# Two feed-forward stages on TensorE: one more pair per group with seven products instead of eight, more low parts made by adding transfers through a load buffer of their own, and the first squares moved

## The chip, the cores and the metric

The kernel runs on one NeuronCore of one Trainium2 chip. The metric is the time of one execution in microseconds (us), as the device measures it. Three runs of the kernel before took 2454.0, 2455.01 and 2455.87 us: median 2455.01. One further execution was profiled; all rows of the trace come from it.

## What is computed

One layer of a streaming encoder block on a residual stream `x` of 256 tokens by 2048 features, in float32:

```python
x = x + 0.5 * swiglu(rms_norm(x, ffn1_norm), ffn1_w_up, ffn1_w_down)
h = rms_norm(x, mix_norm)
...                    # gated recurrence, RG-LRU branch, gates, w_out
x = x + cross_attention(rms_norm(x, xattn_norm), rms_norm(mem, mem_norm), wq, wkv, wo)
x = x + 0.5 * swiglu(rms_norm(x, ffn2_norm), ffn2_w_up, ffn2_w_down)
return rms_norm(x, final_norm)

def swiglu(h, w_up, w_down):
    gate, up = jnp.split(h @ w_up, 2, axis=-1)
    return (jax.nn.silu(gate) * up) @ w_down
```

The change lies in the two feed-forward (SwiGLU) stages; the hidden width is 5632. What stands between them keeps its instructions and gets only other pools for three small tiles.

## The kernel before

**Precision.** TensorE multiplies in float32r, a shortened float32. Each float32 operand is therefore split into a high part `h` (a copy on ScalarE, `split`, L120) and a low part `l` (the raw value minus `h`, on VectorE, L121). A product of two split operands is three matmuls: high by high and high by low (L449, L450), and low by high (L452). 512 columns are written by each.

**Pieces.** The weights arrive from HBM in pieces of 128 by 2048 numbers (1 MB). `plan` lists all of them in their order of use; `weights()` hands out a piece and starts the preparation of the next one, so the program is written one piece ahead of its use. Buffers come in rings: three `raw`, three `h`, three `l` of 2048 columns, and in the feed-forward stages three `wide` ones.

**Groups and pairs.** The hidden features are worked off in 11 groups of 512 (`NG`). For a group, eight up pieces (pairs `p` = 0 to 7) are multiplied with the normed tokens, and their sums make gate and up. A pair is a 2 by 2 block product, for which `PRODUCTS` holds three recipes. `plain` (group 0) and `mixed` use eight products of plain weight blocks, 24 matmuls. `fast` uses seven products, 21 matmuls, and sums of weight blocks: VectorE makes the sums `td` in three operations (L213 to L215), and the sums are split too, into `th` (two copies on ScalarE; the trace calls the tile `h`) and `tl` (two operations on VectorE, 1024 columns each). The tokens' side needs differences (`less`) for `mixed` and sums for `fast`, both from `operand_pairs`/`sums` (L432); `BOTH` lists the pairs that need both.

**Order.** `ffn_order` writes the pieces of a stage. In groups 1 and 2 the pairs alternate between `mixed` and `fast`, four each. From group 3 on the order of pairs is 1, 3, 0, 4, 2, 6, 5, 7, with 0 and 6 `mixed` and the rest `fast`. Behind the pairs of a group stand down pieces of earlier groups (two in groups 1 and 2, then four; 24 matmuls each, always eight pieces for a block of two groups), whose sums are added to the residual (L561). At a group's end VectorE combines the seven sums, activates, and the result is turned on TensorE (L489) and split (`hidop`).

**Added pieces.** For `mixed` pieces after the first one of group 3 VectorE does not make the low part. `begin_added` (L187 to L193) runs one piece earlier: it loads a raw buffer, ScalarE writes `-raw`, rounded, into `l` (L191), and a transfer issued by GpSimd (POOL) adds `raw` to it (L192); `prepare` later copies the high part (L200). There are 15 such pieces in a stage.

**Scheduling.** The framework's scheduler then moves instructions within each engine's queue, TensorE's matmuls too, after costs of its own; each engine runs its queue strictly in the order that results. Only SyncE, ScalarE and VectorE are kept in written order during the first eight pieces. There `head` and `rest` (L600 to L606) say what is done ahead of and behind each piece: loading and splitting the tokens (`head_x`), loading the residual and squaring it on ScalarE (`head_residual`, two column blocks at a time behind pieces 4 and 5), the tokens' sums, and the root of the mean square (`head_rstd`, behind piece 8).

Of the kernel before, what the change touches and what calls it, by code (L numbers as in the profile page):

```python
# [8 lines left out]
F32 = mybir.dt.float32  # L9
# [32 lines left out]
def ffn_order():  # L42

    out, down = [("plain", 0, p) for p in range(8)], [("down", 0, 1, c, 0) for c in range(4)]
    for g in range(1, NG):
        if g < 3:  # L50
            out += [(("mixed", "fast")[p % 2], g, p) for p in (0, 1, 2, 3, 5, 4, 7, 6)]
        else:
            out += [("mixed" if p in (0, 6) else "fast", g, p) for p in (1, 3, 0, 4, 2, 6, 5, 7)]
        if g > 2 and g % 2:
            down = [("down", g - 2, 2, c, b) for c in range(4) for b in (g - 2, g - 1)]
        n = 2 if g < 3 else 4
        out, down = out + down[:n], down[n:]
    return out + [("down", NG - 2, 2, c, b) for c in range(4) for b in (NG - 2, NG - 1)]
# [3 lines left out]
def block_kernel(ctx: ExitStack, tc: tile.TileContext, xT, xin, memT, vec, gfin, bgate, lruw, wu1, wd1, win, wv,  # L62
# [123 lines left out]
    def begin_added(src):  # L186

        raw = rawp.tile([P, 2048], F32, name="raw", tag="raw")
        l = lp.tile([P, 2048], F32R, name="l", tag="l")
        sp.dma_start(raw, src)  # L190
        act.activation(l, raw, ACT.Copy, scale=-1.0)  # L191
        nc.gpsimd.dma_start(l, raw, accum_op=ALU.add)  # L192
        return raw, l  # L193
# [111 lines left out]
    class Squares:  # L305
# [3 lines left out]
        def add(self, src):  # L309
            if self.ss is None:  # L310
                self.ss = small.tile([P, T], F32, name="ss", tag="ss")
                act.activation(self.ss, src, ACT.Square)
            else:
                s = t1("sq")
                act.activation(s, src, ACT.Square)
                dve.tensor_tensor(out=self.ss, in0=self.ss, in1=s, op=ALU.add)

        def rstd(self):
# [5 lines left out]
            r = small.tile([P, T], F32, name="rstd", tag="rstd", bufs=3)  # L324
# [15 lines left out]
    FFN_POOLS = dict(wide=3, hd=1)  # L340

    class TokenSquares:
# [5 lines left out]
        def add(self, c, ts=range(2)):  # L348
            for t in ts:
                name = "hd" if "hd" in scoped else "tmp2"  # L350
                junk = scoped[name].tile([P, 512], F32, name="junk", tag=name)
# [20 lines left out]
    def by_feature(r):  # L372
# [7 lines left out]
        o = small.tile([P, T], F32, name="rstd", tag="rstd", bufs=3)  # L380
# [22 lines left out]
    BOTH = [2, 4]  # L403
    xd = []

    def operand_pairs(src, gain, q, xg, out):

        for a in src:
# [7 lines left out]
            less = None if i else (h[:, 512:768], l[:, 512:768])  # L416
# [7 lines left out]
        def sums(which=((0, "less"), (0, "sums"), (1, "less"), (1, "sums"))):  # L424
            s = slot(name="xs")
            for i, ((h, l), less) in enumerate(out):
# [10 lines left out]
                if (i or 2 * q in BOTH) and (i, "sums") in which:  # L437
                    if not i and len(which) > 1:
                        s = slot(name="xs")
# [148 lines left out]
    def head_residual(i):  # L588
        for c in (2 * i, 2 * i + 1):
            for t in range(2):  # L590
                sp.dma_start(xt[c][:, t * 512:(t + 1) * 512], xin[t * P:(t + 1) * P, c * 512:(c + 1) * 512])
            sq1.add(c)
        if i:
# [11 lines left out]
    for q, i in enumerate((3, 6, 7, 9)):  # L605
        rest[i] = lambda q=q: sums1[q](((0, "less"), (1, "sums")))  # L606
    rest[8] = head_rstd
    for q, i in ((1, 17), (2, 18)):
# [56 lines left out]
    middle.enter_context(scope(tmp=8, tmp2=2, scores=1, extra=2))  # L665
# [523 lines left out]
```

## Time and profile before

| | before |
|---|---|
| median of 3 runs | 2455.01 us (2454.0 to 2455.87) |
| the profiled execution, and its span | 2456.57 us, 2454.8 us |
| granted TensorE clock, mean | 0.997 |
| adding transfers (POOL issues) | 30, of 1024 KB each |
| DMA moved | 507.59 MB, mean 207 GB/s |
| q0 (the adding transfers' queue) | 6.4% of 16 engines' span |
| q1 (the loads' queue) | 53.4% |

The profile names an engine's instruction by its line, what it writes and what it reads. PE is TensorE's matmul, PEld its weight load, DVE is VectorE, ACT is ScalarE, SP is SyncE, which issues the loads. A duration is that of one instruction alone; instructions that follow each other directly overlap by some 0.08 us, so that a chain of them is shorter than its sum. The first feed-forward stage takes up about the first 650 us, the second about the last 700.

### The profile page before, as it was taken

The numbers are of one execution on the slowest core, as the hardware profiler recorded it, in microseconds if no ns is written. First come the engines' busy times: TensorE is split into PE (matmuls) and PEld (weight loads), VectorE is DVE, ScalarE is ACT, GpSimd is POOL, SyncE is SP. The second block draws the span as 40 slices with busy tenths as digits, with TensorE's granted clock in tenths as the row PEclk, the third lists the DMA queues.
The fourth block names the chain that finished last, engine by engine and source line by source line (L and its number), as shares of the span: only waits on it lengthen the run. The fifth ranks groups of instructions, "written<-read, shape, count | busy, mean of one in ns | idle before, by whom it ended". The sixth has DMA issues, their size and how long they took to land.

```text
span 2454.8 us, 30191 instructions
## 1 busy us (share of the span) xinstructions
PE 2434.6 (99%) x12250; PEld 2036.9 (83%) x12250; DVE 1894.1 (77%) x2016; ACT 1391.2 (57%) x1398; POOL 28.3 (1%) x36
## 2 busy tenths in 40 slices
PE   9999999999999999999999999999999999999998
PEld 7887888888888888888888888888888788888887
DVE  6998999999865757567665676556689999999995
ACT  7555666666564454477434554555555566666664
POOL 0000000000000000000000000000000000000000
PEclk9999999999999999999999999999999999999999
DMA  7557777777655445546555555444555677777774
GB/s 278 190 203 234 248 235 235 234 239 239 223 183 194 173 172 180 174 166 228 194 188 177 210 198 189 172 172 155 189 189 189 209 238 239 240 240 235 235 235 152
DMA packets 75020, 507.59 MB, mean 207 GB/s; under 512 B 8320, under 2 KB 8576, under 8 KB 15232
## 3 DMA queue, kind: packets, MB, share of 16 engines
q1 hardware_dynamic: 69840, 473.06, 53.4%
q0 software_dynamic: 4320, 31.46, 6.4%
q8 instruction: 96, 1.57, 0.2%
q10 hardware_dynamic: 720, 1.13, 0.1%
q14 instruction: 44, 0.36, 0.0%
HBM read 472.07 MB, written 2.10 MB: 193 GB/s over the span
## 4 chain that ended last, share of the span: by engine, by line
PE 95%; DVE 2%; ACT 1%; DMA 1%; issue 0%; SPq 0%; ACTq 0%; DVEq 0%
PE acc L449 17%; PE acc L450 17%; PE acc L452 17%; PE acc L231 11%; PE acc L252 8%; PE acc L253 8%; PE acc L255 8%; PE acc L235 5%; DMA raw<-wu 1%; PE acc L489 1%; ACT h L120 1%; DVE l L121 1%; PE acc L389 1%; PE acc L765 0%; PE acc L1048 0%; PE acc L1003 0%
## 5 line engine op out<-in xcount | busy, mean ns | idle before, releaser
L121 DVE TENSOR_TENSOR l<-raw,h 128x2048 fp32r<-128x2048 f32 (+2 forms) x422 | 878.0, 2087 | 364.5 <-ACT h L120 353.0
L120 ACT ACTIVATE h<-raw 128x2048 fp32r<-128x2048 f32 (+2 forms) x422 | 736.7, 1753 | 637.5 <-PE acc L253 204.8
L449 PE MATMUL acc<-h,xh 128*128 128x512 f32 x1280 | 501.2, 392 | 7.1 <-ACT h L120 7.0
L450 PE MATMUL acc<-h,xl 128*128 128x512 f32 x1280 | 499.7, 391 | 0.0
L120 ACT ACTIVATE h<-td 128x1024 fp32r<-128x1024 f32 x224 | 229.6, 1055 | 178.4 <-PE acc L450 131.0
L252 PE MATMUL acc<-h,ops 128*128 128x512 f32 x832 | 326.9, 393 | 0.0
L253 PE MATMUL acc<-h,ops 128*128 128x512 f32 x832 | 324.3, 390 | 0.0
L121 DVE TENSOR_TENSOR tl<-td,h 128x1024 fp32r<-128x1024 f32 x224 | 267.4, 1221 | 33.6 <-ACT h L120 31.0
L449 PEld LDWEIGHTS acc<-h,xh 128*128 128x128 f32 x1280 | 241.7, 189 | 60.0 <-ACT h L120 9.7
L450 PEld LDWEIGHTS acc<-h,xl 128*128 128x128 f32 x1280 | 241.9, 189 | 50.1
L231 PE MATMUL acc<-ops,h 128*128 128x512 f32 x1152 | 278.0, 393 | 0.3
L449 PE MATMUL acc<-h,hidop 128*128 128x512 f32 x704 | 275.7, 392 | 0.0
L450 PE MATMUL acc<-h,hidop 128*128 128x512 f32 x704 | 274.3, 390 | 0.0
L231 PEld LDWEIGHTS acc<-ops,h 128*128 128x128 f32 x1152 | 211.9, 188 | 42.9 <-DVE ops L292 0.9
L452 PE MATMUL acc<-l,xh 128*128 128x512 f32 x832 | 218.9, 390 | 0.0
L255 PE MATMUL acc<-l,ops 128*128 128x512 f32 x832 | 206.1, 390 | 0.0
L452 PE MATMUL acc<-l,hidop 128*128 128x512 f32 x704 | 188.3, 389 | 0.0
L452 PEld LDWEIGHTS acc<-l,xh 128*128 128x128 f32 x832 | 156.5, 188 | 32.6
L255 PEld LDWEIGHTS acc<-l,ops 128*128 128x128 f32 x832 | 156.2, 188 | 32.4
L252 PEld LDWEIGHTS acc<-h,ops 128*128 128x128 f32 x832 | 156.2, 188 | 32.3
L253 PEld LDWEIGHTS acc<-h,ops 128*128 128x128 f32 x832 | 156.3, 188 | 31.6
L452 PEld LDWEIGHTS acc<-l,hidop 128*128 128x128 f32 x704 | 132.2, 188 | 27.5
(220 smaller groups left out, 2347.6 us busy)
## 6 DMA issues: line engine op xcount, KB each, us to landing
raw<-wu SPq DMA_DIRECT2D x172, 1024.0 KB, 4.8
raw<-wd SPq DMA_DIRECT2D x88, 1024.0 KB, 4.8
raw<-win SPq DMA_DIRECT2D x40, 1024.0 KB, 4.8
raw<-wg SPq DMA_DIRECT2D x32, 1024.0 KB, 4.8
l<-raw POOLq DMA_DIRECT2D x30, 1024.0 KB, 7.3
raw<-wab SPq DMA_DIRECT2D x16, 1024.0 KB, 4.8
raw<-wout SPq DMA_DIRECT2D x16, 1024.0 KB, 4.8
raw<-wq SPq DMA_DIRECT2D x16, 1024.0 KB, 4.8
```

The costliest lines, as they stand in the source:

```text
L120: done["high"] = act.activation(h, raw, ACT.Copy).ins
L121: dve.tensor_tensor(out=l, in0=raw, in1=h.bitcast(F32), op=ALU.subtract)
L231: pe.matmul(acc, h[:, k * P:(k + 1) * P], xs[k], start=k == 0, stop=False)
L235: done["product"] = pe.matmul(acc[:, :T], l[:, k * P:(k + 1) * P], xs[k][:, :T], start=False, stop=k == KT - 1).ins
L252: pe.matmul(accs[t], x[:, t * P:][:, :P], h[j], start=first and j == 0, stop=False)
L253: pe.matmul(accs[t], x[:, T + t * P:][:, :P], h[j], start=False, stop=False)
L255: done["product"] = pe.matmul(accs[t], x[:, t * P:][:, :P], l[j], start=False, stop=last and j == 3).ins
L389: pe.transpose(accs[m // 2][:, m % 2 * T + t * P:][:, :P], tile[:, t * 512 + m * P:][:, :P], ident)
L449: pe.matmul(acc, ah, bh, start=start, stop=False)
L450: pe.matmul(acc, al, bh, start=False, stop=False)
L452: pe.matmul(acc, ah, bl, start=False, stop=stop)
L489: pe.transpose(acc[:, z * T + t * P:][:, :P], hid[t][:, (2 * y + z) * P:][:, :P], ident)
```

## The change

`ffn_order` makes one more pair `fast` in each group but the first: in groups 1 and 2 pairs 0, 2 and 6 stay `mixed` (four before), from group 3 on only pair 6 (two before). From group 3 on the order of pairs is now 1, 3, 0, 6, 4, 2, 5, 7. `plan_ffn` marks as `added` every `mixed` piece but pair 0, in groups 1 and 2 as well, and four of the eight down pieces of the blocks that begin at groups 1, 3, 5 and 7, two in a group: 28 added pieces in a stage where there were 15. `begin_added` loads into a pool `own` with one buffer. In the start, the residual's column blocks are loaded and squared one at a time, behind pieces 4, 5, 6 and 7, and the tokens' sums and the root follow behind pieces 7, 8 and 9. Pair 4 needs only sums now (`FAST`), pairs 0 and 2 both kinds. The junk output of the squares takes a `wide` buffer, and `ss`, `rstd` come from a pool of the middle part.

```diff
     for g in range(1, NG):
         if g < 3:
-            out += [(("mixed", "fast")[p % 2], g, p) for p in (0, 1, 2, 3, 5, 4, 7, 6)]
+            out += [("mixed" if p in (0, 2, 6) else "fast", g, p) for p in (0, 1, 2, 3, 5, 4, 7, 6)]
         else:
-            out += [("mixed" if p in (0, 6) else "fast", g, p) for p in (1, 3, 0, 4, 2, 6, 5, 7)]
+            out += [("mixed" if p == 6 else "fast", g, p) for p in (1, 3, 0, 6, 4, 2, 5, 7)]
...
-            kind = "fast" if e[0] == "fast" else "added" if e[0] == "mixed" and e[1:] > (3, 0) else "plain"
+            kind = "fast" if e[0] == "fast" else "plain"
+            if e[0] == "mixed" and e[2]:
+                kind = "added"
+            if e[0] == "down" and 0 < e[1] < NG - 2 and (e[3] + e[4] - e[1]) % 2 == 0:
+                kind = "added"
...
     def begin_added(src):
-        raw = rawp.tile([P, 2048], F32, name="raw", tag="raw")
+        raw = scoped["own"].tile([P, 2048], F32, name="own", tag="own")
         l = lp.tile([P, 2048], F32R, name="l", tag="l")
         sp.dma_start(raw, src)
         act.activation(l, raw, ACT.Copy, scale=-1.0)
...
-    FFN_POOLS = dict(wide=3, hd=1)
+    FFN_POOLS = dict(wide=3, own=1)
...
-    BOTH = [2, 4]
+    BOTH = [0, 2]
+    FAST = [4]
...
-    for i in range(2):
-        rest[4 + i] = lambda i=i: head_residual(i)
...
+    for i in range(3):
+        rest[4 + i] = lambda i=i: head_residual(i)
+    for q, i in enumerate((3, 7, 8, 9)):
+        rest[i] = lambda q=q: sums1[q](((0, "sums" if 2 * q in FAST else "less"), (1, "sums")))
+    made = rest[7], rest[8]
+    rest[7] = lambda: [f() for f in (lambda: head_residual(3), made[0])]
+    rest[8] = lambda: [f() for f in (head_rstd, made[1])]
+    for q, i in ((0, 22), (1, 24)):
         rest[i] = lambda q=q: sums1[q](((0, "sums"),))
```

**Three places in the order.** The first is ScalarE in the first pieces, from the high part of piece 4 on. `junk` are the squares of the residual `x0` to `x3`, `xg` and `xh` the tokens' side. Before:

```order
L120 ACTIVATE h_304<-raw_303 128x2048
L352 ACTIVATE junk_311,sst_103<-x0_99 128x512
L352 ACTIVATE junk_313,sst_103<-x0_99 128x512
L352 ACTIVATE junk_317,sst_103<-x1_100 128x512
L352 ACTIVATE junk_319,sst_103<-x1_100 128x512
L412 ACTIVATE xg_295<-xf_294,vt_76 128x256 x2
L120 ACTIVATE xh_348<-xg_295 128x512
L120 ACTIVATE h_353<-raw_352 128x2048
```

And now:

```order
L120 ACTIVATE h_304<-raw_303 128x2048
L358 ACTIVATE junk_311,sst_103<-x0_99 128x512
L358 ACTIVATE junk_313,sst_103<-x0_99 128x512
L419 ACTIVATE xg_295<-xf_294,vt_76 128x256 x2
L120 ACTIVATE xh_342<-xg_295 128x512
L120 ACTIVATE h_347<-raw_346 128x2048
L358 ACTIVATE junk_354,sst_103<-x1_100 128x512
L358 ACTIVATE junk_356,sst_103<-x1_100 128x512
```

Two squares stand between two high parts where four stood, and the same goes on for pieces 6 and 7. (On SP the first load into `own` now stands ahead of the loads for the third piece.)

The second place is a `fast` piece that is followed by an added one, in a later group of the first stage. ScalarE before (`h_2796`, `h_2800` are the piece's `h` and `th`, `h_2827` is the added piece's high part, `h_2856` belongs to the piece after that):

```order
L120 ACTIVATE h_2796<-raw_2790 128x1536
L120 ACTIVATE h_2800<-td_2792 128x1024 x2
L200 ACTIVATE h_2827<-raw_2785 128x2048
L120 ACTIVATE h_2856<-raw_2850 128x1536
L120 ACTIVATE h_2860<-td_2852 128x1024 x2
```

ScalarE now (`h_2777` is the `th`, `h_2804` the added piece's high part, `h_2833` the next piece's):

```order
L120 ACTIVATE h_2777<-td_2769 128x1024
L204 ACTIVATE h_2804<-own_2762 128x2048
L120 ACTIVATE h_2833<-raw_2827 128x1536
L120 ACTIVATE h_2777<-td_2769 128x1024
L120 ACTIVATE h_2837<-td_2829 128x1024 x2
```

TensorE now, in the same piece (`l_2774`, `tl_2778` its low parts):

```order
L456 MATMUL acc_2738<-h_2777,xh_119 128x512
L457 MATMUL acc_2738<-h_2777,xl_120 128x512
L459 MATMUL acc_2734<-l_2774,xh_119 128x512
L459 MATMUL acc_2735<-l_2774,xh_119 128x512
L459 MATMUL acc_2736<-l_2774,xh_119 128x512
L459 MATMUL acc_2737<-tl_2778,xh_119 128x512
L459 MATMUL acc_2738<-tl_2778,xh_119 128x512
L456 MATMUL acc_2735<-h_2804,xh_387 128x512
L457 MATMUL acc_2735<-h_2804,xl_388 128x512
L456 MATMUL acc_2735<-h_2804,xh_387 128x512
L456 MATMUL acc_2739<-h_2777,xh_119 128x512
L457 MATMUL acc_2739<-h_2777,xl_120 128x512
```

The second half of `th` has moved behind the next high part on ScalarE, which writes the buffer that the piece's own first six matmuls read; on TensorE its matmuls have moved behind the low parts and three matmuls of the added piece. The last piece of each group has the same shape, with a down piece in place of the added one.

The third place is SP at the start of group 3 of the first stage. Before, from the load of pair 1 on (`L207` loads a piece whose low part VectorE makes in one operation, `L210` a `fast` piece, `L190` an added one):

```order
L210 DMA raw_1270<-wu1 128x2048
L210 DMA raw_1314<-wu1 128x2048
L207 DMA raw_1374<-wu1 128x2048
L210 DMA raw_1401<-wu1 128x2048
L190 DMA raw_1441<-wu1 128x2048
L210 DMA raw_1446<-wu1 128x2048
L210 DMA raw_1506<-wu1 128x2048
```

And now (`L194` an added piece):

```order
L194 DMA own_1394<-wu1 128x2048
L214 DMA raw_1290<-wu1 128x2048
L214 DMA raw_1334<-wu1 128x2048
L214 DMA raw_1399<-wu1 128x2048
L214 DMA raw_1459<-wu1 128x2048
L214 DMA raw_1499<-wu1 128x2048
L194 DMA own_1573<-wd1 128x2048
```

The added piece's load stands outside the ring of the three `raw` buffers and ahead of the group's other loads; five `fast` pieces follow each other in the ring where an added one stood among them.

More of the change, by code (lines that the diff above doesn't have):

```diff
@@ L415, in operand_pairs @@
             split(h[:, :512], l[:, :512], g)
-            less = None if i else (h[:, 512:768], l[:, 512:768])
+            less = None if i or 2 * q in FAST else (h[:, 512:768], l[:, 512:768])
             if 2 * q + i in BOTH:
@@ L436, in sums @@
                     made(*less, 2, 0, lambda o: ((a[0], a[1], ALU.subtract), (a[2], a[3], ALU.subtract)))
-                if (i or 2 * q in BOTH) and (i, "sums") in which:
-                    if not i and len(which) > 1:
+                if (i or 2 * q in BOTH + FAST) and (i, "sums") in which:
+                    if not i and less and len(which) > 1:
                         s = slot(name="xs")
@@ L586, in head_x, with head_residual @@
         pairs1.append(out[-1])
[L588 to L593, printed above, removed]
+    def head_residual(c):
+        for t in range(2):
+            sp.dma_start(xt[c][:, t * 512:(t + 1) * 512], xin[t * P:(t + 1) * P, c * 512:(c + 1) * 512])
+        sq1.add(c)
+        if c == 3:
             sp.dma_start(vt[:, small_n:NVEC], vec[:, small_n:])
     head += [lambda p=p: head_x(p) for p in range(8)]
-    for i in range(2):
-        rest[4 + i] = lambda i=i: head_residual(i)
     rstd1 = []
```

18 lines of the change are left out of this document (8 added, 10 removed).

## The prediction, made blind

> **What bounds the kernel now.** I read the page's busy shares and chain first, then the table by windows, the list of what PE waited for, and the timelines of the two feed-forward stages. The chain of waits is PE almost throughout:
>
> ```profile
> PE 2434.6 (99%) x12250; PEld 2036.9 (83%) x12250; DVE 1894.1 (77%) x2016; ACT 1391.2 (57%) x1398; POOL 28.3 (1%) x36
> PE 95%; DVE 2%; ACT 1%; DMA 1%; issue 0%; SPq 0%; ACTq 0%; DVEq 0%
> 762.12 1.81 PE acc L255 x8
> 767.56 1.81 PE acc L255 x8
> ```
>
> The last two rows, from the chain in order of time, are one place in two neighbouring pieces of 24 matmuls: 5.44 us, so 0.2267 us for a matmul of 512 columns. A matmul less is worth that wherever PE does not wait. The windows show where it does, and how full DVE is there (columns: PE, weight load, DVE, ACT, POOL busy, clock, DMA share):
>
> ```profile
> 0.00:50.00 50.00, 45.83 (x200) 37.95 (x200) 27.38 (x46) 39.48 (x72) 0.20 (x4) 0.97 0.79 298
> 50.00:100.00 50.00, 49.41 (x221) 40.70 (x222) 49.03 (x59) 32.06 (x30) 0.00 (x0) 1.00 0.58 210
> 150.00:200.00 50.00, 46.63 (x199) 37.05 (x198) 44.71 (x48) 25.94 (x23) 1.00 (x1) 0.97 0.58 196
> 1900.00:1950.00 50.00, 46.97 (x203) 38.13 (x203) 44.03 (x41) 29.77 (x25) 0.87 (x1) 0.97 0.66 218
> 265.66:327.75 62.09, 62.09 (x279) 51.50 (x279) 57.34 (x56) 38.36 (x32) 1.76 (x2) 1.00 0.74 243
> ```
>
> The last row is one whole later group of the first stage: PE never idle, DVE busy 57.34 of 62.09 us. The period is that of the adding transfers:
>
> ```profile
> 289.13 0.89 POOL L192 DMA_DIRECT2D l<-raw  x1 [45.19 <-ACT l L191]
> 351.22 0.86 POOL L192 DMA_DIRECT2D l<-raw  x1 [45.09 <-ACT l L191]
> ```
>
> So PE sets the end, but in these stages DVE is 92% full, and the change gives DVE more and PE less. The few waits of PE, in brackets:
>
> ```profile
> 42.09 0.66 PE L449 MATMUL acc<-h,xh 128*128 128x512 f32 x1 [2.50 <-ACT h L120]
> 50.59 0.50 PE L449 MATMUL acc<-h,xh 128*128 128x512 f32 x1 [1.17 <-ACT h L120]
> 183.08 0.50 PE L449 MATMUL acc<-h,xh 128*128 128x512 f32 x1 [0.36 <-ACT h L120]
> 191.41 0.50 PE L449 MATMUL acc<-h,xh 128*128 128x512 f32 x1 [3.02 <-ACT h L120]
> 1928.36 0.73 PE L452 MATMUL acc<-tl,xh 128*128 128x512 f32 x2 [3.03 <-DVE tl L121]
> 42.00:44.00 2.00, 1.91 (x5) 1.52 (x6) 1.93 (x1) 0.04 (x1) 0.00 (x0) 0.57 0.00 0
> 44.00:46.00 2.00, 2.00 (x7) 1.58 (x6) 1.48 (x6) 0.42 (x1) 0.00 (x0) 0.58 0.23 29
> 192.00:194.00 2.00, 2.00 (x7) 1.62 (x6) 1.97 (x4) 0.57 (x1) 0.00 (x0) 0.62 1.00 422
> 194.00:196.00 2.00, 2.00 (x6) 1.52 (x6) 1.80 (x2) 1.54 (x2) 0.00 (x0) 0.53 0.53 143
> ```
>
> After 2.50 and 3.02 us of idleness the granted clock is near half for some 4 us (0.57, 0.58; 0.62, 0.53), which costs 0.425 x 3.9 = 1.66 and 0.38 x 2 + 0.47 x 2 = 1.70 us more. The wait at 50.59, 1.17 us long, has no such sequel. I take 1.7 for the one at 1928 too. Price of all waits: head 2.50 + 1.17 + 1.66 = 5.3; first stage 0.36 + 3.02 + 1.70 = 5.1; second stage 3.03 + 1.7 = 4.7; together 15.1 us.
>
> **Products.** Seven instead of eight means 21 matmuls instead of 24. Groups 1 and 2 get one more such pair each, groups 3 to 10 one more each: 10 a stage, 20 in all, 60 matmuls fewer: 60 x 0.2267 = **-13.6 us**. This term I hold for sure, since the diff's table says it outright.
>
> **DVE in a later group.** The rows for the operations, and one seven-product piece from its first operation to that of the next (298.25 to 304.78 us, 6.53 us):
>
> ```profile
> 298.25 1.22 DVE L213 TENSOR_TENSOR td<-raw 128x1024 f32<-128x1024 f32 x1
> 304.78 1.22 DVE L213 TENSOR_TENSOR td<-raw 128x1024 f32<-128x1024 f32 x1
> 269.00 4.49 DVE L121 TENSOR_TENSOR l<-raw,h 128x2048 fp32r<-128x2048 f32 x2 [0.52 <-ACT h L120]
> ```
>
> Two low parts in a row take 4.49, so 2.2 each. A group gains one seven-product piece (the one it replaces had its low part added by a transfer, DVE nothing) and loses two low parts of down pieces: 57.34 + 6.53 - 2 x 2.2 = 59.5 us of DVE, against 62.09 - 0.68 = 61.4 of PE: 97%. On the average it fits, with 1.9 us to spare. But the order within a group counts. A seven-product piece keeps PE 4.76 us and DVE 6.53, so a run of them puts DVE behind: before, at most two in a row (3.5 us), now three and then four (5.3 and 7.1). The eight-product piece gives back 5.4. The four down pieces keep PE 21.8 us and DVE 2 x 2.2 plus the 57.34 - 6 x 6.53 - 4 x 2.2 = 9.4 us of epilogue, turn and residual, so they give back 8. The balance closes in every group; what is asked for is 3.6 us more of lead. ACT's durations:
>
> ```profile
> L120 ACT ACTIVATE h<-td 128x1024 fp32r<-128x1024 f32 x76 | 77.1, 1055 | 55.0 <-PE acc L450 55.0
> L120 ACT ACTIVATE h<-raw 128x1536 fp32r<-128x1536 f32 x38 | 56.7, 1492 | 65.7 <-issue 36.2 <-PE acc L450 29.5
> L120 ACT ACTIVATE h<-raw 128x2048 fp32r<-128x2048 f32 x28 | 52.9, 1913 | 32.3 <-PE acc L450 32.3
> ```
>
> The tightest places are the two shown in the order: the second half of the sums' high part stands on ACT behind the next piece's high part, which waits for the buffer that PE frees with its sixth matmul. In the third piece: 6 x 0.2267 = 1.36, then 1.49 and 1.06 on ACT: 3.91 us after the piece's start. PE has 18 matmuls to do before it needs it, 4.08 us: covered by 0.17. At the last piece of a group the copy in front is 2048 wide: 1.36 + 1.91 + 1.06 = 4.33, against 20 matmuls, 4.53: covered by 0.2. The cover is PE's work from the next piece, pulled forward. Without it PE needs the half after 10 matmuls, 2.27 us, and waits 1.64 and 2.06, 3.7 us a group. DVE's own stretch from the eight-product piece's end on comes to the same: it starts the low part when that buffer is free, and finishes the fourth piece's last half about when PE asks. With margins of 0.2 us and hand-overs between engines of some 0.05 each, I take 0.4 us of waiting a group, nearest to the covered end: 16 groups, **+6.4 us** (bounds 0 and 16 x 3.7 = 59).
>
> **Costed at nothing.** ACT copies each added down piece twice, 1.9 more, and the new seven-product piece takes 1.49 + 2 x 1.06 = 3.6 where the one it replaces took two copies, 3.8: 38.4 + 3.6 = 42 of 61.4 us in a group, hidden in ACT's idle time; without that cover 3.6 a group. On SP a load into the new buffer waits for the last piece's copy out of it, and raw loads stand behind it; they fill buffers that are used about ten us later. POOL has nothing behind its transfers here. Squares take a wide buffer instead of one of their own, at the stages' ends and in the head, where no sums of weights are alive; and the moved pools add no instruction.
>
> **Head.** Squares of the residual stood four in a row on ACT, between high parts:
>
> ```profile
> 15.86 1.98 PE L452 MATMUL acc<-l,xh 128*128 128x512 f32 x8
> 13.82 2.18 ACT L120 ACTIVATE h<-raw 128x512 fp32r<-128x512 f32 x4
> 27.20 0.18 ACT L352 ACTIVATION_READ_ACCUMULATOR junk<-x 128x1 f32 x1
> 29.55 0.89 ACT L412 ACTIVATE xg<-xf,vt 128x256 f32<-128x256 f32 x2
> 30.48 0.63 ACT L120 ACTIVATE xh<-xg 128x512 fp32r<-128x512 f32 x1
> 31.02 1.91 ACT L120 ACTIVATE h<-raw 128x2048 fp32r<-128x2048 f32 x1
> 36.61 1.28 ACT L362 ACT_TABLE_LOAD   x1
> 38.74 1.28 ACT L603 ACT_TABLE_LOAD   x1
> 40.15 1.89 ACT L120 ACTIVATE h<-raw 128x2048 fp32r<-128x2048 f32 x1
> L352 ACT ACTIVATE junk<-x 128x512 f32<-128x512 f32 x40 | 25.0, 625 | 30.7 <-DVE x L561 27.8 <-DVE x L956 2.7
> ```
>
> From 31.02 to 40.15 two pieces' high parts are 9.1 us apart where PE uses a piece in 5.44: hence the wait at 42.09. Now two squares follow each high part, and the root with its tables comes after all eight: 0.89 + 0.63 + 1.91 + 2 x (0.63 + 0.18) = 5.0 us of ACT a piece, inside 5.44. Both waits and the slow clock go, 5.3. Against that, SP now issues the first load into the new buffer ahead of the third piece's, 1 MB at the first window's 298 GB/s: 3.5 us. That piece's copies began at 13.82, and PE came to it after the eight matmuls from 15.86 on, at 17.7: a lead of 3.9, now almost used up. I book 0.8 for it: **-4.5 us** (0 to -5.3).
>
> **Start of group 3.** Both 3 us waits trace back to late loads, in the chain:
>
> ```profile
> 178.49 10.33 DMA raw<-wu
> 1915.19 10.65 DMA raw<-wu
> 175.62 12.67 SPq L210 DMA_DIRECT2D raw<-wu  x3
> l<-raw POOLq DMA_DIRECT2D x30, 1024.0 KB, 7.3
> ```
>
> Three loads stand behind each other on SP (12.67 us), because the piece with the adding transfer holds one of three raw buffers for two pieces' time, while that transfer (7.3 us) moves its own data. With a buffer of its own the others rotate over three again, and loads go out a piece earlier. What is late next is DVE: 49.0 of 50 us busy from 50 to 100, and group 3 now opens with three seven-product pieces. I count 8 of 9.8 us: **-8 us** (0 to -9.8); and for DVE's lag in groups 1 and 2, where the deferred sums now fall (and one more set of them), **+2** (0 to +5).
>
> **Sum.** -13.6 + 6.4 - 4.5 - 8 + 2 = -17.7. The profiled execution took 2456.57 us, 1.77 more than its span; the median of the runs is 2455.01, 1.56 less. 2455.0 - 17.7 = **2437 us**.
>
> **Rivals.** *Everything is hidden*: all waits go and DVE costs nothing: -13.6 - 15.1 = -28.7, 2426 us. For it: PE did not idle once from 52 to 183 us with DVE full. *The waits only change their name*: late loads become late DVE operations, and of the gain the products are left: -13.6 + 6.4 + 2 = -5.2, 2450. *DVE becomes the bound* (slower): the pulled-forward matmuls do not cover the copies, each later group waits 3.7 us: -13.6 - 4.5 - 8 + 59 + 2 = +35, 2490; it decides from (13.6 + 4.5 + 8 - 2) / 16 = 1.5 us a group. For it: 97% and margins of 0.2. Against: the balance closes in each group, so lateness does not add up. In the Trainium skill, "TensorE: Matmul & The Clock Gate", Part 1, the clock falls only after an idle window of about 3.4 us, so by that page waits of 2 us stay at 2490. The trace differs: 2.50 us sufficed here, 1.17 did not; if 2.06 does, 16 x 1.7 = 27 us more. *The adding transfers come late*: three a group from one buffer. The nearest deadline is the first down piece's: free buffer, copy and transfer end some 5 us ahead of its use. Landing in twice 7.3 us would cost 2.4 a group, +39 - 17.7 = +21, 2476. The DMA share, 0.74 in the group, has room for a third transfer.
>
> **How the numbers follow.** Forecast 0.53 (its own range 2429 to 2446), everything hidden 0.14, waits renamed 0.16 (half of it beyond the bound of faster), DVE bound 0.13 (a quarter of it mild enough to end near no change), late transfers 0.04. A measurement of this kernel tells 0.2%, 4.9 us, from no change. Faster: 0.53 + 0.14 + 0.08 = 0.75; same: 0.08 + 0.03 = 0.11; slower: 0.10 + 0.04 = 0.14. The range, 2424 to 2458, leaves out the slower cases and a little below the best one.
>
> **What would show it.** A group's period of 61.4 to 61.9 us between equal adding transfers bears out the DVE step; 63 or more makes the third rival. No idle PE over 1 us before 60 us, and the clock at 1.00 there, bears out the head. No load with ten microseconds to landing at group 3, and no PE wait of 3 us, bears out the buffer. DVE's share in a group should be 0.96 to 0.97. The forecast is wrong if PE waits for DVE's l or tl, or ACT's h, in every group.

## The result, and the profile after

The change did nothing that can be measured: 2454.88 us (median, 2453.66 to 2457.44) against 2455.49 for the kernel before on the same chip, ratio 0.9997 (95% interval 0.9988 to 1.0006). 2437 had been predicted, 17.9 us less. The profiled execution's span is 2453.2 us (2454.8 before).

In the changed kernel's code L194 is the load into `own`, L195 ScalarE's first copy out of it, L196 the adding transfer, L204 the high part; the matmuls are L456, L457 (high) and L459 (low), the turn is L496. The page's busy times, its chain of waits and its row of adding transfers:

```profile
PE 2429.5 (99%) x12190; PEld 2018.4 (82%) x12190; DVE 1911.0 (78%) x2094; ACT 1467.6 (60%) x1464; POOL 50.8 (2%) x62
PE 83%; DVE 6%; DMA 4%; ACT 4%; issue 3%; SPq 0%; ACTq 0%; POOLq 0%; DVEq 0%
l<-own POOLq DMA_DIRECT2D x56, 1024.0 KB, 8.2
```

The 60 matmuls are gone (12250 to 12190), yet TensorE's busy time fell by 5.1 us, not 13.6, and its share of the chain from 95% to 83%. The windows (same columns as before the change):

```profile
0.00:50.00 50.00, 48.54 (x219) 40.73 (x220) 31.84 (x61) 39.57 (x72) 0.20 (x4) 1.00 0.92 340
50.00:100.00 50.00, 49.62 (x221) 40.05 (x220) 47.91 (x51) 39.19 (x37) 1.87 (x2) 1.00 0.74 231
150.00:200.00 50.00, 45.07 (x196) 35.34 (x195) 47.00 (x48) 31.70 (x28) 1.73 (x2) 1.00 0.61 205
1900.00:1950.00 50.00, 47.47 (x203) 37.95 (x202) 44.37 (x45) 32.85 (x27) 2.03 (x3) 0.97 0.73 230
535.43:597.53 62.10, 62.02 (x276) 50.66 (x275) 58.63 (x59) 41.74 (x35) 2.62 (x3) 1.00 0.80 258
```

The start is better (48.54 busy for 45.83, clock 1.00), the stretch at group 3 is worse, and a whole later group, the last row, still takes 62.1 us with three matmuls fewer (276 for 279): TensorE is called busy there, but its matmuls stand further apart. What TensorE waited for (total, times, longest):

```profile
PE acc L459 <- DMA l<-own: 5.6, 3, 3.1
PE acc L459 <- DVE l L121: 4.0, 3, 2.4
PE acc L456 <- ACT h L120: 1.8, 5, 0.8
```

The waits for ScalarE and for late sums are replaced by waits for the adding transfer and for a low part on VectorE. In TensorE's timeline the longest of each kind, first the wait for the low part, at group 2, then the one for the transfer, at group 3:

```profile
156.60 1.20 PE L459 MATMUL acc<-l,hidop 128*128 128x512 f32 x4 [2.40 <-DVE l L121]
...
208.14 0.73 PE L459 MATMUL acc<-l,hidop 128*128 128x512 f32 x2 [3.09 <-DMA l<-own]
```

Different chains lead to them. Ahead of the row at 156.60, in order of time (start, duration, what):

```profile
129.54 1.87 ACT l L195
131.41 0.35 issue
131.76 11.68 DMA l<-own
143.44 0.02 SPq L194
...
143.49 0.33 SPq L194
...
143.91 6.87 DMA raw<-wu
...
150.87 1.49 ACT h L120
152.35 0.62 ACT ev L488
...
153.00 0.75 DVE ev L489
...
154.35 0.06 DVE l L121
```

The load into `own` waits on SP until the transfer out of the same buffer has landed, 11.68 us; the raw load in the next place of SP's queue goes out 0.42 us later, with no wait of its own; ScalarE, in order, stands before the high part from that raw buffer, with VectorE's epilogue and low part behind. All of SP's waits of this kind in the change, and under them those of `e5_poolshead` (below), which has the same single buffer and 30 adding transfers:

```profile
SPq L194 <- DMA l<-own: 474.0, 54, 13.3
```

```profile
SPq L190 <- DMA l<-own: 67.1, 21, 9.8
```

This total is not a price by itself: in the kernel `g3_firstdown` below it is still 444.4 us, and TensorE waits for no transfer there. As far as these runs show, it costs only where what stands behind on SP is needed soon. Before the row at 208.14 stand ScalarE's copy and the transfer itself:

```profile
194.90 1.90 ACT L195 ACTIVATE l<-own 128x2048 fp32r<-128x2048 f32 x1
```

```profile
197.15 10.94 DMA l<-own
```

This buffer's load had been issued at 176.61 and had landed at 181.3, so SP holds nothing up here. But the copy stands behind the last piece's high part on ScalarE (further ahead in later groups), and TensorE wants the piece at 204.9, one matmul after its last one at 204.66: 7.8 us after the transfer starts, and it took 10.94. Finally the place where a later group loses time (weight loads of TensorE, and ScalarE's timeline):

```profile
574.12 0.19 PEld L456 LDWEIGHTS acc<-h,xh 128*128 128x128 f32 x1 [0.50 <-ACT h L120]
```

```profile
570.68 1.06 ACT L120 ACTIVATE h<-td 128x1024 fp32r<-128x1024 f32 x1 [1.43 <-DVE td L217]
571.65 1.47 ACT L120 ACTIVATE h<-raw 128x1536 fp32r<-128x1536 f32 x1
573.03 1.04 ACT L120 ACTIVATE h<-td 128x1024 fp32r<-128x1024 f32 x1
```

That is the third piece of a group: the second half of its sums (573.03) stands behind the next high part (571.65), as the order had shown, and TensorE is held up until the half is done at 574.1. By the second matmul behind it TensorE is 0.35 us late. A second place of this shape, with the half at 554.23, costs 0.08 us; some 40 further matmuls of the group stand 4 to 9 ns further apart than before, and what sets this is not shown.

To see where time goes I compare the stretches between turns (starts of the first matmul of each turn, L489 or L496, in the timelines of TensorE; us). "Start and buffer" is the kernel `e5_poolshead` below:

| from turn to turn | before | start and buffer | change |
|---|---|---|---|
| start to 0 | 61.62 | 56.53 | 56.65 |
| 0 to 1 | 52.84 | 54.20 | 53.43 |
| 1 to 2 | 51.89 | 51.89 | 55.67 |
| 2 to 3 | 58.10 | 52.39 | 58.43 |
| 3 to 4 | 62.13 | 62.13 | 62.69 |
| 4 to 5 | 62.09 | 62.09 | 62.33 |
| 8 to 9 | 62.09 | 62.09 | 62.11 |
| second stage, 2 to 3 | 57.02 | 52.04 | 56.42 |

### The profile page after: what moved, and what is told of

The parts are those of the page before. It is cut to its first block, busy times and chain, and to the rows that moved or that the text cites. A ratio compares the mean times of both kernels' runs of the same rounds, so it can differ in the third digit from the quotient of the medians.

```text
span 2453.2 us, 30276 instructions
## 1 busy us (share of the span) xinstructions
PE 2429.5 (99%) x12190; PEld 2018.4 (82%) x12190; DVE 1911.0 (78%) x2094; ACT 1467.6 (60%) x1464; POOL 50.8 (2%) x62
## 4 chain that ended last, share of the span: by engine, by line
PE 83%; DVE 6%; DMA 4%; ACT 4%; issue 3%; SPq 0%; ACTq 0%; POOLq 0%; DVEq 0%
PE acc L456 14%; PE acc L457 13%; PE acc L459 13%; PE acc L235 11%; PE acc L256 8%; PE acc L257 8%; PE acc L259 8%; PE acc L239 5%; ACT h L120 3%; DMA l<-own 3%; DVE l L121 2%; DVE tl L121 1%; DVE td L217 1%; DMA raw<-wu 1%; PE acc L496 1%
## 5 line engine op out<-in xcount | busy, mean ns | idle before, releaser
L121 DVE TENSOR_TENSOR l<-raw,h 128x2048 fp32r<-128x2048 f32 (+2 forms) x396 | 809.1, 2046 | 350.3 <-ACT h L120 342.8
L120 ACT ACTIVATE h<-raw 128x2048 fp32r<-128x2048 f32 (+2 forms) x396 | 679.4, 1719 | 499.3 <-PE acc L257 205.6
L456 PE MATMUL acc<-h,xh 128*128 128x512 f32 x1260 | 493.2, 394 | 3.1 <-ACT h L120 1.8
L457 PE MATMUL acc<-h,xl 128*128 128x512 f32 x1260 | 487.9, 390 | 0.0
L120 ACT ACTIVATE h<-td 128x1024 fp32r<-128x1024 f32 x264 | 275.1, 1054 | 209.8 <-PE acc L457 95.8
L121 DVE TENSOR_TENSOR tl<-td,h 128x1024 fp32r<-128x1024 f32 x264 | 319.3, 1219 | 17.5 <-ACT h L120 17.4
L456 PEld LDWEIGHTS acc<-h,xh 128*128 128x128 f32 x1260 | 236.5, 188 | 66.6 <-ACT h L120 17.2
L456 PE MATMUL acc<-h,hidop 128*128 128x512 f32 x704 | 276.9, 393 | 0.0
L457 PEld LDWEIGHTS acc<-h,xl 128*128 128x128 f32 x1260 | 236.6, 188 | 47.4
L457 PE MATMUL acc<-h,hidop 128*128 128x512 f32 x704 | 275.0, 391 | 0.0
L459 PE MATMUL acc<-l,xh 128*128 128x512 f32 x732 | 198.3, 390 | 1.9 <-DVE l L121 1.6
L459 PE MATMUL acc<-l,hidop 128*128 128x512 f32 x704 | 189.7, 391 | 7.7 <-DMA l<-own 5.3
L459 PEld LDWEIGHTS acc<-l,xh 128*128 128x128 f32 x732 | 137.2, 188 | 31.6 <-DVE l L121 2.4
L459 PEld LDWEIGHTS acc<-l,hidop 128*128 128x128 f32 x704 | 132.0, 188 | 36.8 <-DMA l<-own 6.2
```

Source lines behind the costliest of these rows:

```text
L120: done["high"] = act.activation(h, raw, ACT.Copy).ins
L121: dve.tensor_tensor(out=l, in0=raw, in1=h.bitcast(F32), op=ALU.subtract)
L456: pe.matmul(acc, ah, bh, start=start, stop=False)
L457: pe.matmul(acc, al, bh, start=False, stop=False)
L459: pe.matmul(acc, ah, bl, start=False, stop=stop)
```

## The experiments

**The parts that were forecast as gains.** The spread squares alone, on the kernel before:

```diff
-    for i in range(2):
-        rest[4 + i] = lambda i=i: head_residual(i)      # two column blocks
+    for i in range(3):
+        rest[4 + i] = lambda i=i: head_residual(i)      # one column block
...
+    rest[7] = lambda: [f() for f in (lambda: head_residual(3), made[0])]
+    rest[8] = lambda: [f() for f in (head_rstd, made[1])]
```

> The kernel before with the spread squares alone. Theory A (the gain of the start is real and stands by itself; it was spent elsewhere in the changed kernel): both waits at 42 and 50 us go, the clock stays at 1.00 there, the first group's turn comes 5 us earlier as in the changed kernel (56.65 against 61.62), and the whole ends 5 us earlier, 2450 us. Rival B (a lead won at the start is lost at the next place where VectorE is late, so it never reaches the end): the first turn is early, but group 2 or 3 waits longer by as much, 2455 us.

Measured 2451.22 us, ratio 0.9982 (0.9973 to 0.9991): 4.1 us less. The first turn came at 56.30, 5.3 us earlier, and but for 1.3 us between turns 0 and 1 the gain reached the end. Theory A. The load buffer with the moved pools alone, on the kernel before:

```diff
-        raw = rawp.tile([P, 2048], F32, name="raw", tag="raw")
+        raw = scoped["own"].tile([P, 2048], F32, name="own", tag="own")
...
-    FFN_POOLS = dict(wide=3, hd=1)
+    FFN_POOLS = dict(wide=3, own=1)
```

> The kernel before with the load buffer of its own for added pieces and the moved pools alone; 15 added pieces a stage, old kinds and orders. Theory A (the 3 us waits at group 3 were late raw loads, and the buffer cures them when there are few added pieces): no raw load of 10 us near 178 and 1915 us, no wait over 1 us there, 8 us less, 2447 us. Rival B (VectorE or ScalarE is late at group 3 anyway): the loads are early, the waits stay under the name of l, tl or h, 2454 to 2456 us.

Measured 2447.27 us, ratio 0.9967 (0.9955 to 0.9980): 8.1 us less. The turns 2 and 3 were 52.39 and 52.08 us apart in the two stages, 10.7 us less in all; the first turn came 1.3 us later, at 62.93. Theory A. Both together:

> The kernel before with the load buffer and pools of its own and the spread squares: the whole change but its products, kinds and orders. Theory A (the two gains are independent, 4.1 and 8.1 us measured apart): 2443 us, first turn at 56 to 57 us, no wait over 1 us at group 3. Rival B (what is won at the start is lost at group 3, or both won the same time): 2447 us. By A the rest of the change, forecast at 13.6 us less, costs 12 us.

Measured 2442.07 us, ratio 0.9947 (0.9931 to 0.9964): 13.4 us less, the sum within 1.2. What TensorE waited for in it, whole:

```profile
PE warm L109 <- DVE ones L106: 1.1, 1, 1.1
PE acc L451 <- ACT h L120: 0.4, 1, 0.4
```

So the remaining part of the change, kinds, orders and 26 more adding transfers, costs 12.8 us where 5.2 less were forecast. All that follows looks for these 18 us.

**Fewer adding transfers.** The block of down pieces that begins at group 1 plain, then all down pieces plain:

```diff
-            if e[0] == "down" and 0 < e[1] < NG - 2 and ...
+            if e[0] == "down" and 1 < e[1] < NG - 2 and ...    # e3; NG < e[1] in e4
```

> The changed kernel with the down pieces of the block that begins at group 1 plain (24 added pieces a stage, not 28). Theory A (the wait of 3.1 us at 205 us and that of 2.2 us at 1940 us with the slow clock behind it are adding transfers that come late): both go, some 7 us; VectorE gets 4.4 us more in groups 3 and 4, of which 1 to 2 us show in each: 2450 to 2452 us. Rival B (VectorE is late there, and the transfer only shares the time): the waits stay under the name of l or tl and grow, 2455 to 2460 us.

> The changed kernel with all down pieces plain, 12 fewer adding transfers a stage. Theory A (the later groups wait for ScalarE and VectorE, and VectorE has 58.6 of 62.07 us): VectorE needs 58.6 + 2 x 2.2 = 63.0 us a group, so the period goes to 63.5 or more in 8 groups a stage, +20 to +30 us less the 7 us of the late transfers: 2470 us or so. Rival C (the adding transfers and the loads get in each other's way, and that costs the 0.66 us a group): the period falls to 61.4 to 61.7 us and the late transfers go, 2440 us.

e3: 2455.14 us, ratio to before 0.9999 (0.9990 to 1.0009), as the change. The waits for the transfer at group 3 went (2 to 3: 54.69 and 52.51 us), as A has it, but 4 to 5 grew to 64.69 and, in the second stage, 64.19: TensorE waited 1.77 and 1.32 us for the next block's first transfer. The time is rival B's, its mechanism (VectorE late at group 3) is not what came. e4: 2459.26 us, ratio 1.0015 (1.0006 to 1.0025). Its later group:

```profile
471.50:534.34 62.84, 62.18 (x274) 50.26 (x273) 62.13 (x62) 39.04 (x32) 0.86 (x1) 1.00 0.65 218
```

VectorE is busy 62.13 of 62.84 us: it is the bound here, 0.7 us a group more than in the change. So the transfers do take off VectorE what they should; theory A in kind, with less of a loss than expected (4.4 us in all, not 15): the period is 62.84 us, not 63.5 or more. Between turns 2 and 3 the stretches fell to 55.25 and 52.55 us, since the late transfers went too.

**The deferred sums.** They fall among seven-product pieces of group 2 in the change.

```diff
-    for q, i in ((0, 22), (1, 24)):
+    for q, i in ((0, 26), (1, 27)):
```

> The changed kernel with the two deferred sums of the tokens made behind pieces 26 and 27 (down pieces) in place of 22 and 24 (among seven-product pieces of group 2). Theory A (the 5 us more of waits in groups 1 and 2 of the first stage than of the second are VectorE making these sums): the waits up to the turn at 166 us fall by 3 us or more, 2451 to 2452 us. Rival B (VectorE is behind from the start on, and the sums only show it): they move into group 3, 2454 to 2456 us.

Measured 2448.73 us, ratio to before 0.9974 (0.9964 to 0.9983): 6.2 us less than the change, more than the 3 to 4 that A expected. Turns 1 and 2 are 51.73 us apart (55.67). ScalarE's copy out of `own` is 3.6 us earlier, and the transfer (timeline of POOL) starts at

```profile
128.19 0.89 POOL L196 DMA_DIRECT2D l<-own  x1 [25.64 <-ACT l L195]
```

not 131.76; it lands at 137.05, after 8.86 us for 11.68, and the raw load behind it on SP goes out at 137.52 in place of 143.91. The sums cost little by themselves; they stood ahead of the copy that starts this chain.

**The copies within a piece.** The high part of the sums in one copy, VectorE as it was (`f2b_thact`, shown); then VectorE's low part in one operation too (`f2_thwhole`, `split(th, tl, td)` in place of the loop):

```diff
-        for a in (0, 1024):
-            split(th[:, a:a + 1024], tl[:, a:a + 1024], td[:, a:a + 1024])
+        done["high"] = act.activation(th, td, ACT.Copy).ins
+        for a in (0, 1024):
+            dve.tensor_tensor(out=tl[:, a:a + 1024], ...)
```

> The changed kernel with the high part of the weight sums copied by ScalarE in one operation of 2048 columns, not two of 1024; VectorE as in the change. Theory A (the 0.66 us a later group is the second half standing behind the next piece's high part): that place goes, the period falls from 62.07 to 61.5 to 61.7 us, 2447 to 2451 us. Rival B (VectorE is behind in the runs of seven-product pieces, and whatever ScalarE does comes after it): one copy must wait for all four sums, the period is 62.1 us or more, 2455 to 2462 us.

> As the kernel with one copy on ScalarE, and VectorE makes the low part of the sums in one operation of 2048 columns too (2.2 us for 2 x 1.14, so VectorE has 0.5 to 1 us less a group). Theory A: as with the one copy, within 2 us of it. Rival B (VectorE's load sets the period): clearly faster than the one copy alone, by 0.5 us a group, 7 us or more.

2717.99 and 2683.48 us: 263 and 229 us more than the change, as no theory had it. The wait of TensorE for the one copy, and VectorE's for it in every piece:

```profile
PE acc L457 <- ACT h L224: 135.6, 77, 2.7
```

```profile
589.77 2.36 DVE L226 TENSOR_TENSOR tl<-td,h 128x1024 fp32r<-128x1024 f32 x2 [2.06 <-ACT h L224]
```

With halves VectorE and ScalarE work on the two sides of a piece at the same time; with one copy they take turns, 8.56 us a piece (581.21 to 589.77 between two such rows) for 6.53 in the kernel before. As a test of the place it is inconclusive, since it brought a larger wait of its own.

**Order, lead and VectorE's load**, all on the kernel with the sums moved (2448.73 us):

```diff
-  (1, 3, 0, 6, 4, 2, 5, 7)
+  (1, 3, 0, 4, 6, 2, 5, 7)                                        # g1
-  if e[0] == "down" and ...:
+  if e[0] == "down" and ... and e[1:] != (1, 2, 0, 1):            # g3
-  for o, n, x in ((e0, 1, e0), (e1, 3, e1), (e1, 2, e1)):
+  for o, n, x in ((e0, 1, e0),):                                  # g5
-  for o, n, x in ((e3, 6, e2), (e2, 3, e2)):
+  for o, n, x in ((e3, 6, e2),):                                  # g5
```

> The kernel with the sums behind pieces 26 and 27 (2448.7 us), with the eight-product pair of groups 3 to 10 fifth, not fourth: order 1, 3, 0, 4, 6, 2, 5, 7, so the runs of seven-product pieces are four and then three. Theory A (the 0.66 us a group hangs on one place, the third piece, whose second half stands behind the next high part): in this order the inversion falls on another piece, and the loss a group changes by 0.2 us or more either way: 2443 to 2446 us, or 2452 and more. Rival B (VectorE's lag at the end of a run, whatever the place): the same total of runs, the period stays within 0.1 us of 62.07, 2447 to 2450 us.

> The kernel with the sums behind pieces 26 and 27 (2448.7 us), with the first down piece of group 3 plain, one of 28 added pieces fewer a stage. Theory A (the first adding transfer for a down piece comes late in group 3 because ScalarE's copy stands later there, and only that one): the waits at 199 and 1934 us (2.6 us with 1.7 of slow clock, 2.2 us) go and the later groups stay: 2443 to 2445 us. Rival B (the lateness is a lack of lead that moves on, as when the whole block was made plain): the wait turns up at the next added piece or as VectorE's l, 2447 to 2450 us.

> The kernel with the sums behind pieces 26 and 27, with three of the additions at a group's end left out (the sums for gate and up lack the parts of three accumulators): VectorE has 3 x 0.69 = 2.1 us less in each group, nothing else changes. Theory A (the 0.66 us a later group is the order on ScalarE within a piece): the period stays at 62.0 to 62.1 us, 2447 to 2449 us. Rival B (VectorE's lag over the group): the period falls to 61.5 us, 2438 to 2441 us.

g1: 2450.44 us (ratio to before 0.9978, 0.9969 to 0.9988); g3: 2442.47 (0.9944, 0.9929 to 0.9958); g5: 2442.99 (0.9947, 0.9932 to 0.9962). A later group in g1, then in g5:

```profile
532.16:593.79 61.63, 61.63 (x276) 50.63 (x275) 58.26 (x59) 41.73 (x35) 2.61 (x3) 1.00 0.83 267
```

```profile
525.32:587.42 62.10, 62.02 (x276) 50.65 (x275) 56.73 (x56) 41.74 (x35) 2.62 (x3) 1.00 0.81 259
```

With 1.9 us less of VectorE the period is the same 62.10; with another order it is 61.63 at nearly the same load. So the later groups lose by the order of the work, not by VectorE's sum: theory A twice by the period, though neither time is in A's range. g1 lost it again in group 3 (59.35 and 57.26 us between turns 2 and 3, for 58.10 and 54.63). g5, whose sums for gate and up are incomplete, gained 5.7 us all the same, 4.9 of it between turns 2 and 3 of the two stages, where ScalarE's copy out of `own` came 2.5 us earlier (186.91 for 189.37). g3 took the wait at group 3 away (54.02 and 52.57 us) and nothing came in its place: theory A.

**Each alone on the change, and all three together.** h4 has only the plain piece, h3 only the new order, from group 4 on, h1 both and the moved sums.

> The changed kernel with only the first down piece of group 3 plain. Theory A (the transfer is late by itself, whatever VectorE does in groups 1 and 2): 2454.9 - 6.3 = 2448.6 us, as much as the same edit won with the sums moved. Rival B (with VectorE late from the deferred sums its low part is late instead): 2452 to 2455 us.

> The changed kernel with only the eight-product pair fifth from group 4 on; sums and down pieces as in the change. Theory A: the period of later groups is 61.62 us, the waits of groups 1 to 3 stay: 2454.9 - 6.3 = 2448.6 us. Rival B (the lead that the order wins is used up by the late transfers ahead of it): 2452 to 2455 us.

> The changed kernel with all three places mended: deferred sums behind pieces 26 and 27, the first down piece of group 3 plain, and from group 4 on the eight-product pair fifth. Theory A (three separate losses): 2442.5 us with two of them, less 14 groups x (62.07 - 61.62) = 6.3 us: 2436 us, which would be the forecast of 2437 for the change itself. Rival B (one lack of lead that only moves): 2440 to 2445 us, with new waits in groups 4 and 5.

h4: 2447.75 us, ratio to before 0.9967 (0.9954 to 0.9981), 7.1 less than the change: A. One plain piece is worth all that e3's four were to give. h3: 2452.07 us, ratio 0.9985 (0.9976 to 0.9994): later groups at 61.62 us as A says, but 63.37 between turns 4 and 5 in both stages, so that 2.8 us stay of 6.3, which is rival B's time. h1: 2447.77 us, ratio 0.9969 (0.9958 to 0.9981), not 2436, and more than B's 2445: later groups at 61.62, but 68.36 and 67.45 us between turns 3 and 4 (62.1 without the new order). ScalarE there, and TensorE:

```profile
268.32 1.92 ACT L195 ACTIVATE l<-own 128x2048 fp32r<-128x2048 f32 x1 [6.79 <-DMA own<-wd]
270.14 1.90 ACT L120 ACTIVATE h<-raw 128x2048 fp32r<-128x2048 f32 x1
```

```profile
278.10 1.22 PE L459 MATMUL acc<-l,hidop 128*128 128x512 f32 x2 [3.10 <-DVE l L121]
```

The transfer of 251.94 landed at 263.33, the next load went out at 263.38 and landed at 268.21; from 261.5 on ScalarE stood before its copy, with the plain piece's copy, whose load had long landed, behind. Rival B in its effect, with SP held by the landing as at group 2 in the change.

**Two load buffers**, on the change (k1), on h1 (k4) and on g1 (k2):

```diff
-    slots = pool("slots", 24)
+    slots = pool("slots", 22)
-    FFN_POOLS = dict(wide=3, own=1)
+    FFN_POOLS = dict(wide=3, own=2)
```

> The changed kernel with two buffers for added loads in place of one (the room comes from the slots, 22 in place of 24). Theory A (the wait of 3.1 us at group 3 is ScalarE's copy coming late and a slow transfer behind it, its load had landed 13 us earlier; the single buffer only blocks ScalarE's queue afterwards, where nothing waits for it in this order): the 7.6 us that ScalarE stands before the copy at 213 us go, PE's waits stay, 2453 to 2456 us. Rival B (the single buffer makes the transfers late): the waits at 205 and 1940 us go, 2445 to 2449 us.

> The kernel with all three places mended (2447.8 us; new waits of 3.3 us on a low part of VectorE at 275 and 2010 us, with slow clock behind them) with two buffers for added loads. Theory A (in group 4 ScalarE's copy out of the single buffer stood 6.8 us at the head of its queue, for the transfer before to land and the next load to come, and the plain down piece's copy stood behind it): these waits go, 2447.8 - 2 x 6 = 2436 us, and later groups stay at 61.6 us. Rival B (the lead is missing on VectorE, whatever the buffers): 2444 to 2448 us.

> The kernel with the eight-product pair fifth from group 3 on and the sums behind pieces 26 and 27 (2450.4 us; all 28 added pieces) with two buffers for added loads. Theory A (the same 6.8 us of ScalarE behind the single buffer, in group 3, cost 3.1 us at 216 us and as much in the second stage, with the slow clock): 2450.4 - 3.2 - 4 = 2443 us; the waits at the start of group 3 (2.1 and 0.4 us for high parts) stay. Rival B: they stay or move, 2448 to 2451 us.

2456.05 us (ratio 1.0001, 0.9991 to 1.0010), 2450.40 (0.9978, 0.9968 to 0.9987) and 2455.50 (0.9999, 0.9989 to 1.0009). On the change itself (k1) the waits for the transfer at group 3 shrank but stayed, as A has it: 2.41 us for 3.09 (58.81 us between turns 2 and 3) and, in the second stage, 1.42 for 2.24, there without a slow clock behind it (54.03 us for 56.42). The wait at 156.60 went: 52.33 us between turns 1 and 2 for 55.67. In k4 the stretch between turns 3 and 4 fell from 68.36 to 62.23 us (then 63.71 for 61.57), so the single buffer was that wait's cause: A for the place, not for the whole. In k2 the waits of 2.90 us at 216 and 3.00 at 1950 for a low part are gone, so A has the place right. But the high parts at the start of group 3 came later (2.53 us of waiting for 1.96) and so did the transfer (1.20 for 0.57): between turns 2 and 3 3.1 us were won in the second stage (54.19 for 57.26) and 0.4 in the first (58.96 for 59.35). k4's and k2's times are above both theories'. All three lost 6.6 to 6.9 us between turns 0 and 1 (60.03, 60.23 and 61.25 for 53.43, 53.31 and 54.35 with one buffer), and about 1 us in the middle part. SP still waited for landings:

```profile
SPq L194 <- DMA l<-own: 477.4, 52, 13.4
```

This is k1's row, for 474.0 us in the change: a second buffer lets the load into it stand a piece earlier in SP's queue, where it waits for a transfer all the same, raw loads behind. The loss between turns 0 and 1 may come of this, but the 22 slots were not tried by themselves, so its cause is open.

**Only the products of groups 1 and 2**, with the sums moved; old kinds and order from group 3, down pieces plain:

```diff
-            out += [("mixed" if p == 6 else "fast", g, p) for p in (1, 3, 0, 6, 4, 2, 5, 7)]
+            out += [("mixed" if p in (0, 6) else "fast", g, p) for p in (1, 3, 0, 4, 2, 6, 5, 7)]
...
```

> The kernel with the sums behind pieces 26 and 27, with the old kinds and order from group 3 on (pairs 0 and 6 of eight products, added) and all down pieces plain: of the products, only the four in groups 1 and 2 are left. Theory A (the loss sits in groups 3 to 10, and four seven-product pieces more in groups 1 and 2 are worth their matmuls): 2442.1 - 4 x 0.68 = 2439.4 us, period 62.09 us in later groups. Rival B (a fifth and sixth seven-product pair in groups 1 and 2 puts VectorE behind, and group 3 pays for it): 2442 to 2445 us.

Measured 2440.35 us, ratio to before 0.9936 (0.9922 to 0.9951), within 1 us of A, and the fastest of all kernels here: 16 us less than the kernel before on the same chip.

## Why the prediction was wrong

- **Products** (-13.6): 60 matmuls went, as said. Groups 1 and 2 keep their gain (52.18 and 51.61 us between turns in the second stage of the kernel with the sums moved, for 52.80 and 52.08). In the later groups it was given back.
- **Head** (-4.5): right, 4.1 measured alone.
- **Start of group 3** (-8): 8.1 measured for the buffer alone, but as 10.7 us won between turns 2 and 3 of the two stages less 1.3 lost at the start, so that the close agreement is in part luck. In the change the late raw loads were gone too, but another wait of the same size stood there, so the rival that waits only change their name described this place.
- **The step that failed** is "costed at nothing": the loads, copies and transfers of the added pieces have no term in the sum, and at two places they cost. *On SP* it says that a load into the new buffer waits for the last piece's copy out of it, and that the raw loads behind fill buffers used ten us later. The load waits for the landing of the adding transfer that reads that buffer, 6.9 to 12.8 us after its start, and every raw load written behind it waits too; at group 2 the lead of ten us was not there. Set against the kernel with start and buffer, the change lost 3.8 us between turns 1 and 2, and both an earlier copy (f3) and a second buffer (k1) take this away. *At group 3* the first down piece's transfer is late without SP: its copy, held to be hidden in ScalarE's idle time, stands in that engine's queue until 194.90. Here the change lost 6.0 and 4.4 us between turns 2 and 3 of the two stages; making this one piece plain takes back 3.7 and 3.9 of them (h4, with 1.6 more between turns 1 and 2), a second buffer leaves most of the waits (k1). Both places together: 14.2 us, where -2.0 for products, +2 for VectorE's lag and +0.8 of waits had been booked: 13.4 of the 18 us. How much of the wait at group 3 comes from the late start and how much from a slow transfer is open: at the median of 8.2 us it would have landed at 205.4, 0.5 us late, not 3.09.
- **The rival of late transfers** was named, but as a price of 2.4 us in every group, with 0.04, and argued from the DMA share. Its 5 us in hand are right for a later group: the transfer for the first down piece starts 12.8 us ahead of its use there (569.66 for 582.5) and lands 4.9 ahead. What came was local: at group 3 it starts 7.8 ahead.
- **Steady waits** (0.4 a group): the place was right, the size too small. A period of 62.07 against 61.41 is 0.66 a group, some 0.4 of it at the two places of the shape that the order had shown, and it eats the 0.68 that three matmuls are worth. The margins of 0.17 and 0.2 us were worked out from ScalarE waiting for TensorE's sixth matmul; in the row at 570.68 it waited for VectorE's `td`, which comes later. Over the 14 groups behind group 3 that is 3.6 of the 18 us.
- **VectorE** at 59.5 us: 58.63 measured, and it did not bind (g5); the rival at +35 fell. Without the added down pieces it would have been the bound (e4).

All three mends together did not add up (h1). So part of these losses is one lead handed on, and the new order's 6 us more in the group behind the plain piece are explained only as far as the single buffer goes (k4).

## What to carry to other kernels

Here a buffer that a transfer reads was held until the transfer landed, not only until the engines had copied it (landing at 143.44, the next load at 143.49), and the load into it, on a queue that serves others in order, stopped them all for that time. So ask of each new buffer who stands behind its refill, on the load queue and on the engine that copies it, and give the longest landing, not the median, against the lead of the worst group, not of the steady one. Split a change with several gains in it and measure the parts: here two of them were worth 13.4 us by themselves, and the third hid that.

## What the runs showed of the hardware

The length of an idle stretch does not tell whether the clock falls. The waits of 3.09 us at 205 and of 2.24 us at 1940, in one execution (the second in TensorE's timeline; windows behind both, where the third last column is the granted clock):

```profile
1942.46 0.73 PE L459 MATMUL acc<-l,hidop 128*128 128x512 f32 x2 [2.24 <-DMA l<-own]
```

```profile
208.00:210.00 2.00, 1.86 (x8) 1.57 (x9) 0.00 (x0) 0.00 (x0) 0.00 (x0) 1.00 0.38 74
210.00:212.00 2.00, 2.00 (x11) 1.65 (x10) 0.29 (x1) 0.00 (x0) 0.00 (x0) 1.00 0.94 397
...
1944.00:1946.00 2.00, 2.00 (x6) 1.59 (x5) 0.00 (x0) 0.00 (x0) 0.00 (x0) 0.50 0.90 369
```

The longer had no sequel, the shorter was followed by half clock; in h3 a wait of 1.90 us at 205 was too (0.50 from 209 to 211). The Trainium skill, "TensorE: Matmul & The Clock Gate", Part 1, says that activity is judged in windows that run freely, and the two rows are in keeping with that. Its idle time of about 3.4 us is not borne out here, since 1.90 sufficed. At the prediction's estimate of 1.7 us for such a stretch, a difference of that size between two kernels here can come of this alone. A wait also costs more than itself without any change of clock: behind the one at 574.12 the first matmul took until 574.46, 0.34 us for the usual 0.227. Adding transfers of the same 1 MB took between 6.9 and 12.8 us in the change; what sets this was not tried.
